# Clearing tiles on ScalarE, mixing whole stores with half-batch stores, and moving the last two output slots to plain transfers

## The chip, the core and the metric

One core of a Trainium2 chip runs the whole program. The metric is device time in microseconds (us) of one execution, as the median of several runs. The granted clock was 1.00 in all of them. Before the change the median was 195.56 us in the first three runs. Of the sixteen DMA engines, which move the data, "landing" means here the moment at which one of them counts its part of a transfer as done; "engine-us" are microseconds summed over the sixteen.

## The reference

The program cuts overlapping 8x8 windows, stride 4, out of 16 images of 64 channels of 64x64 floats. Nothing is computed; it is copying alone.

```python
x: (16, 64, 64, 64) float32            # 16.8 MB read
n_h = n_w = (64 - 8) // 4 + 1          # 15
result: (16, 15, 15, 64, 8, 8)         # 59.0 MB written
for i in range(n_h):
    for j in range(n_w):
        result[:, i, j] = x[:, :, 4*i : 4*i + 8, 4*j : 4*j + 8]
```

Seen as memory, the output is 3600 rows (16 images x 15 x 15 windows) of 16 KB each: one window of one image, all channels.

## The kernel before

The input is loaded once into a tile `L`. Partition `p` holds one half of the channels (`ch`, 64 partitions each), one half of the images (`y`, "half-batch"), one image and one quarter of the rows (`q = p & 3`). A quarter of 16 rows gives four windows, called slots `s` = 0 to 3, for each column `j`. Slot 3 needs four rows of the next partition, which VectorE fetches with a shuffle.

```python
for y in range(NY):                       # loads, 24 in all
    for q in range(HQ):
        load(nc.sync, 0, y, q, SMALL, CL)     # 28 of 32 channels, on SyncE's queue
        load(nc.gpsimd, 0, y, q, 0, SMALL)    # 4 channels, on GpSimd's queue
        load(nc.gpsimd, 1, y, q, 0, CL)       # the other channel half
```

Four tiles `G` of 128 partitions x 16 KB turn. ScalarE (`act`) and VectorE (`dve`) copy windows into one, then GpSimd issues one indirect store of its 128 rows. The row numbers are in an index tile. A row whose index lies out of bounds is dropped.

```python
def scatter(g, ix, j, s):
    st = nc.gpsimd.indirect_dma_start(out=o_v, out_offset=...(ap=ix[:, 0:1]), in_=g..., 
                                      bounds_check=B * NWIN - 1, oob_is_err=False)
...
EARLY = 3
for t in range(NG):                       # clear what a half-store does not fill
    for half in range(CH):
        nc.vector.memset(G[t][...32 partitions..., :, :, :], 0.0)
t = 0
for y in range(NY):                       # half-stores: 64 of 128 rows valid
    for j in range(EARLY):
        ...fill...; scatter(G[t % NG], (idx_y0, idx_y1)[y], j, 0); t += 1

units = [(j, s) for j in range(NW) for s in (0, 2) if s or j >= EARLY]
for j, s in units:
    g = G[t % NG]; t += 1
    if s == 0:                            # "whole" store: slots 0 and 1
        ...; scatter(g, idx, j, s)
    else:                                 # "crossed" store: slots 2 and 3
        turn = j % 2                      # which half of the partitions holds slot 3
        fill(g, turn, s, j, 0, HP, (act, act))
        fill(g, 1 - turn, s + 1, j, 0, HP, (dve, dve))
        scatter(g, (idx_hi, idx_lo)[turn], j, s)
```

Slot 3 of the last quarter does not exist, so a crossed store drops 16 rows. All of them lie in partitions 64 to 127 with `idx_hi` and in 0 to 63 with `idx_lo`.

## Time and profile before

| | before |
|---|---|
| median | 195.56 us (195.54 to 195.88) |
| span of the profiled run | 193.9 us |
| VectorE, ScalarE, GpSimd busy | 68%, 64%, 27% |
| moved | 75.81 MB, 391 GB/s over the span |
| loads end / last 16 KB record ends / span ends | 47.2 / 190.6 / 193.9 us |

The way to read it: no compute engine is near full, and the DMA row is at nine tenths almost throughout. So the useful question is not what a copy costs but where the sixteen DMA engines stand idle. The prediction below shows the lines. Three more matter for what follows. They are SyncE's own waits; the columns are who waited for whom, us in total, times, and the longest. L204 is the end of the program.

```profile
SPq L204 <- DMA out_dram<-G,idx: 160.6, 1, 160.6
SPq L204 <- DMA out_dram<-G,idx_hi: 4.5, 1, 4.5
SPq L204 <- PEq L204: 2.5, 2, 2.0
```

SyncE waits for all stores, and then, in the last line, another 2.0 us for the other engines at the final barrier.

### The profile page before, as it was taken

The numbers are of one execution on the slowest core, as the hardware profiler recorded it, in microseconds if no ns is written. First come the engines' busy times: TensorE is split into PE (matmuls) and PEld (weight loads), VectorE is DVE, ScalarE is ACT, GpSimd is POOL, SyncE is SP. The second block draws the span as 40 slices with busy tenths as digits, with TensorE's granted clock in tenths as the row PEclk, the third lists the DMA queues.
The fourth block names the chain that finished last, engine by engine and source line by source line (L and its number), as shares of the span: only waits on it lengthen the run. The fifth ranks groups of instructions, "written<-read, shape, count | busy, mean of one in ns | idle before, by whom it ended". The sixth has DMA issues, their size and how long they took to land.

```text
span 193.9 us, 478 instructions
## 1 busy us (share of the span) xinstructions
DVE 131.9 (68%) x156; ACT 123.5 (64%) x66; POOL 53.3 (27%) x54
## 2 busy tenths in 40 slices
DVE  6887778995999998766577657774777477643000
ACT  0000008960999999999779677977797779772000
POOL 7402211106463233231404211331323232311000
DMA  2999999999989999999999999999999999999980
GB/s 85 326 408 401 402 399 397 400 400 405 426 333 382 406 419 419 423 423 404 426 433 421 416 419 419 423 423 433 423 416 412 426 423 423 426 416 421 412 345 30
DMA packets 11476, 75.81 MB, mean 391 GB/s; under 512 B 3776, under 2 KB 3776, under 8 KB 7872
## 3 DMA queue, kind: packets, MB, share of 16 engines
q0 software_dynamic: 9616, 68.43, 85.9%
q1 hardware_dynamic: 1856, 7.34, 9.8%
q14 instruction: 4, 0.03, 0.0%
HBM read 16.78 MB, written 69.21 MB: 444 GB/s over the span
## 4 chain that ended last, share of the span: by engine, by line
DMA 66%; DVE 17%; issue 6%; POOL 2%; POOLq 1%; DVEq 0%; PEldq 0%
DMA out_dram<-G,idx 21%; DMA L<-in_x_dram 18%; DMA out_dram<-G,idx_hi 14%; DMA out_dram<-G,idx_lo 12%; DVE G L136 8%; DVE G L139 6%; DVE G L138 3%; POOL L L57 2%; POOLq L204 1%; DVEq L136 0%; POOL pi L68 0%; DVEq L138 0%; PEldq L204 0%
## 5 line engine op out<-in xcount | busy, mean ns | idle before, releaser
L136 ACT COPY G<-L 64x2048 f32<-64x2048 f32 (+1 forms) x65 | 122.2, 1896 | 22.5 <-DMA out_dram<-G,idx 9.9
L136 DVE COPY G<-L 64x2048 f32<-64x2048 f32 (+1 forms) x37 | 44.8, 1221 | 15.6 <-DMA out_dram<-G,idx 12.7
L139 DVE STREAM_SHUFFLE G<-L 64x1024 f32<-64x1024 f32 x30 | 38.3, 1275 | 0.0
L138 DVE COPY G<-L 64x1024 f32<-64x1024 f32 x30 | 20.7, 690 | 20.1 <-DMA out_dram<-G,idx_hi 13.3
L150 DVE MEMSET G<- 32x4096 f32 x8 | 27.8, 3472 | 7.9 <-issue 6.2
L115 POOL DMA_INDIRECT out_dram<-G,idx x12 | 12.4, 1030 | 33.3 <-ACT G L136 33.3
L115 POOL DMA_INDIRECT out_dram<-G,idx_hi x8 | 11.8, 1471 | 31.4 <-DVE G L139 17.8
L136 ACT ACT_TABLE_LOAD x1 | 1.3, 1283 | 29.6 <-DMA L<-in_x_dram 29.6
L57 POOL DMA_DIRECT2D L<-in_x_dram x16 | 9.8, 626 | 25.0 <-DMA L<-in_x_dram 24.4
L115 POOL DMA_INDIRECT out_dram<-G,idx_lo x7 | 9.7, 1390 | 20.5 <-ACT G L136 14.3
L115 POOL DMA_INDIRECT out_dram<-G,idx_y x6 | 9.3, 1547 | 13.7 <-DVE G L136 8.8
L77 DVE TENSOR_TENSOR th<-tc,tq 128x1 int32<-128x1 int32 x2 | 0.3, 159 | 0.1
L77 DVE CUSTOM_DVE_ANT_0 idx_y<-idx,th 128x2 uint16<-128x2 uint16 x2 | 0.3, 158 | 0.1
L74 DVE TENSOR_SCALAR th<-tc 128x1 int32<-128x1 int32 x2 | 0.3, 154 | 0.1
L68 POOL IOTA pi<- 128x1 int32 x1 | 0.1, 125 | 0.4 <-PEq L204 0.4
L139 DVE LOAD_MASK_SELECT G<-L x30 | 0.2, 6 | 0.0
L77 DVE CUSTOM_DVE_ANT_0 idx_hi<-idx,th 128x2 uint16<-128x2 uint16 x1 | 0.2, 159 | 0.0
L77 DVE CUSTOM_DVE_ANT_0 idx_lo<-tb,th 128x2 uint16<-128x2 uint16 x1 | 0.2, 159 | 0.0
L77 DVE CUSTOM_DVE_ANT_0 idx<-tb,th 128x2 uint16<-128x2 uint16 x1 | 0.2, 161 | 0.0
L77 DVE CUSTOM_DVE_ANT_0 idx_lo<-idx_lo,th 128x2 uint16<-128x2 uint16 x1 | 0.2, 158 | 0.0
L77 DVE CUSTOM_DVE_ANT_0 tb<-tb,th 128x2 uint16<-128x2 uint16 x1 | 0.2, 159 | 0.0
L91 DVE TENSOR_SCALAR th<-th 128x1 int32<-128x1 int32 x1 | 0.2, 153 | 0.0
(13 smaller groups left out, 1.7 us busy)
## 6 DMA issues: line engine op xcount, KB each, us to landing
L<-in_x_dram POOLq DMA_DIRECT2D x8, 1024.0 KB, 21.1
L<-in_x_dram SPq DMA_DIRECT2D x8, 896.0 KB
L<-in_x_dram POOLq DMA_DIRECT2D x8, 128.0 KB, 21.3
out_dram<-G,idx POOLq DMA_INDIRECT x12, 14.6
out_dram<-G,idx_hi POOLq DMA_INDIRECT x8, 13.9
out_dram<-G,idx_lo POOLq DMA_INDIRECT x7, 14.1
out_dram<-G,idx_y POOLq DMA_INDIRECT x6, 6.2
```

The lines of the kernel that those rows point to most:

```text
L57: eng.dma_start(out=L[p0 : p0 + QP - HQ + 1 : HQ, c0:c1, :, :], in_=x_v[ch, y, q, :, c0:c1, :])
L68: nc.gpsimd.iota(pi[:, :], pattern=[[0, 1]], base=0, channel_multiplier=1)
L74: nc.vector.tensor_scalar(out=d[:, :], in0=a[:, :], scalar1=float(m), scalar2=None, op0=ALU.mult)
L77: nc.vector.tensor_tensor(out=d[:, :], in0=a[:, :], in1=b[:, :], op=op)
L91: nc.vector.tensor_scalar(out=th[:, :], in0=th[:, :], scalar1=-1.0, scalar2=FAR, op0=ALU.mult, op1=ALU.add)
L115: st = nc.gpsimd.indirect_dma_start(out=o_v, out_offset=bass.IndirectOffsetOnAxis(ap=ix[:, 0:1], axis=0), in_=g.rearrange("p c r w -> p (c ...
L136: copy(out=g[d, cs, :, :], in_=L[f, :, s * ST : s * ST + WS, cols])
L138: copy(out=g[d, cs, 0:ST, :], in_=L[f, :, s * ST : RB, cols])
L139: nc.vector.stream_shuffle(out=g[d, cs, ST:WS, :], in_=L[f, :, 0:ST, cols], mask=nxt)
L150: nc.vector.memset(G[t][p0 : p0 + QP, :, :, :], 0.0)
L204: with _tile.TileContext(nc) as tc:
```

## The change

Three things are meant to save time: free VectorE of 27.8 us of clearing so that the first stores issue earlier; put whole stores between the half-stores of the second half-batch so that the DMA has more to do while ScalarE and VectorE are short of time; and let the last two slots leave as plain transfers from SyncE, sixteen rows at a time. Besides, the choice of the half that drops rows goes from 8 `idx_hi` and 7 `idx_lo` to 9 and 6. (`HWP = 8` covers all loads, so the loads are the same.)

```diff
-    EARLY = 3
-    for t in range(NG):
-        for half in range(CH):
-            nc.vector.memset(G[t][p0 : p0 + QP, :, :, :], 0.0)
+    EARLY = NG - 1
+    zero = ipool.tile([P, 1], f32, name="zero")
+    nc.vector.memset(zero[:, :], 0.0)
+    for g in G:
+        act(out=g.rearrange("p c r w -> p (c r w)"), in_=zero.to_broadcast([P, CFREE]))
...
-            turn = j % 2
+            turn = int(crossed % 5 in (1, 3))
+            crossed += 1
...
+    for j in range(EARLY):
+        part(0, j)
+    plain = [(j, 0) for j in range(EARLY, NW - 1)]
+    cross = [(j, 2) for j in range(NW)]
+    for j in range(EARLY):
+        part(1, j)
+        unit(*plain.pop(0))
+    while plain:
+        for w in cross[:2]:
+            unit(*w)
+        cross = cross[2:]
+        unit(*plain.pop(0))
+
+    j = NW - 1
+    tile_()                                   # one tile is passed over
+    for s in range(2):
+        g = tile_()
+        ...four copies into partitions 32 to 95...
+        for q in range(HQ):
+            free(nc.sync.dma_start(out=o_q[q * NSLOT + s, j], in_=g_q[QP + q : ... : HQ]))
```

More of the change, by code (lines that the diff above doesn't have):

```diff
@@ L50 @@
     x_v = x.rearrange("(y b) (ch cl) (hq r) w -> ch y hq b cl (r w)", y=NY, ch=CH, hq=HQ)
-    SMALL = 4
+    SMALL, HWP = 4, 8
     def load(eng, ch, y, q, c0, c1):
@@ L104 @@
         for q in range(HQ):
-            load(nc.sync, 0, y, q, SMALL, CL)
-            load(nc.gpsimd, 0, y, q, 0, SMALL)
+            hw = y * HQ + q < HWP
+            if hw:
+                load(nc.sync, 0, y, q, SMALL, CL)
+            load(nc.gpsimd, 0, y, q, 0, SMALL if hw else CL)
             load(nc.gpsimd, 1, y, q, 0, CL)
@@ L112, with free @@
     G = [gpool.tile([P, C, WS, WS], f32, name=f"G{n}") for n in range(NG)]
+    o_q = out.rearrange("b i j c r w -> i j b (c r w)")
+    def free(st):
+        tc.declare_no_dep(st.ins, group="stores", reason="each store writes rows of its own")
+        tc.add_to_no_dep_group("stores", st.ins)
     def scatter(g, ix, j, s):
@@ L123, in scatter @@
         )
-        tc.declare_no_dep(st.ins, group="stores", reason="each store writes rows of its own")
-        tc.add_to_no_dep_group("stores", st.ins)
+        free(st)
     def fill(g, half, s, j, lo, n, copies):
@@ L141, with tile_, part, unit @@
     act, dve = nc.scalar.copy, nc.vector.tensor_copy
-    EARLY = 3
-    assert EARLY < NG
-    for t in range(NG):
-        for half in range(CH):
-            p0 = half * HP + (QP if t < EARLY else 0)
-            nc.vector.memset(G[t][p0 : p0 + QP, :, :, :], 0.0)
-    t = 0
-    for y in range(NY):
-        for j in range(EARLY):
-            for half in range(CH):
-                copies = (dve, dve) if y and half and j == 1 else (act, dve)
-                fill(G[t % NG], half, half, j, y * QP, QP, copies)
-            scatter(G[t % NG], (idx_y0, idx_y1)[y], j, 0)
-            t += 1
-    units = [(j, s) for j in range(NW) for s in (0, 2) if s or j >= EARLY]
-    for j, s in units:
-        g = G[t % NG]
-        t += 1
+    EARLY = NG - 1
[3 more added lines that the diff above has]
+        act(out=g.rearrange("p c r w -> p (c r w)"), in_=zero.to_broadcast([P, CFREE]))
+    at = 0
+    def tile_():
+        nonlocal at
+        at += 1
+        return G[(at - 1) % NG]
+    def part(y, j):
+        g = tile_()
+        for half in range(CH):
+            fill(g, half, half, j, y * QP, QP, (dve, dve) if y and half else (act, dve))
+        scatter(g, (idx_y0, idx_y1)[y], j, 0)
+    crossed = 0
+    def unit(j, s):
+        nonlocal crossed
+        g = tile_()
         if s == 0:
             for half in range(CH):
-                fill(g, half, s + half, j, 0, HP, (act, dve))
+                fill(g, half, half, j, 0, HP, (act, dve))
             scatter(g, idx, j, s)
         else:
-            turn = j % 2
+            turn = int(crossed % 5 in (1, 3))
+            crossed += 1
             fill(g, turn, s, j, 0, HP, (act, act))
@@ L173 @@
             scatter(g, (idx_hi, idx_lo)[turn], j, s)
+    for j in range(EARLY):
[13 more added lines that the diff above has]
+    for s in range(2):
+        g = tile_()
+        cols = slice(j * ST, j * ST + WS)
+        for y in range(NY):
+            d = slice(QP + y * QP, QP + (y + 1) * QP)
+            for ch, copy in enumerate((act, dve)):
+                f = slice(ch * HP + y * QP, ch * HP + (y + 1) * QP)
+                copy(out=g[d, ch * CL : (ch + 1) * CL, :, :], in_=L[f, :, s * ST : s * ST + WS, cols])
+        g_q = g.rearrange("p c r w -> p (c r w)")
+        for q in range(HQ):
+            free(nc.sync.dma_start(out=o_q[q * NSLOT + s, j], in_=g_q[QP + q : QP + q + (B - 1) * HQ + 1 : HQ]))
 _INS = ['x', 'window_size', 'stride']
```

## The prediction

> **What bounds the kernel now.** First the page: busy time of the engines, the slices (the DMA row is the mean busy share, in tenths, of the sixteen DMA engines in 40 slices of 4.85 us), and the chain of work that ended last:
>
> ```profile
> DVE 131.9 (68%) x156; ACT 123.5 (64%) x66; POOL 53.3 (27%) x54
> ...
> DMA  2999999999989999999999999999999999999980
> ...
> DMA packets 11476, 75.81 MB, mean 391 GB/s; under 512 B 3776, under 2 KB 3776, under 8 KB 7872
> ...
> DMA 66%; DVE 17%; issue 6%; POOL 2%; POOLq 1%; DVEq 0%; PEldq 0%
> ```
>
> No compute engine passes 68%, and the DMA engines sit at nine tenths from the second slice to the last but one: the kernel is bound by moving 75.8 MB. What is left to win is idle time of the DMA engines, so I next asked the view of windows for DMA share (last column but one; over 1.00 where records overlap) by stage:
>
> ```profile
> 2.30:5.30 3.00, 2.83 (x1) 0.00 (x0) 3.00 (x6) 1.00 0.57 178
> 5.30:47.00 41.70, 33.87 (x34) 12.27 (x7) 8.19 (x13) 1.00 1.04 394
> 47.00:54.00 7.00, 5.85 (x5) 5.95 (x4) 4.00 (x3) 1.00 1.02 424
> 54.00:56.00 2.00, 1.94 (x3) 1.98 (x2) 1.35 (x2) 1.00 0.67 271
> 56.00:73.00 17.00, 16.69 (x25) 16.81 (x10) 5.32 (x5) 1.00 0.96 400
> 73.00:187.00 114.00, 70.13 (x91) 86.52 (x46) 30.29 (x24) 1.00 1.01 421
> 187.00:191.00 4.00, 0.00 (x0) 0.00 (x0) 0.00 (x0) 1.00 0.32 135
> ```
>
> Loads run to 47 us, stores from there. There are only two holes that this change can touch. One is at 54 to 73 us, where ACT and DVE are full (16.8 of 17 us) and the DMA is not. Summing the packet records per microsecond gives 22.5 engine-us missing from 16 engines between 54 and 73 us, that is **1.4 us**. The other is 187 to 191 us, where half the engines have ended.
>
> GpSimd's row of the timeline (start us, us, what, and the idle time before it), then the group of instructions that clears tiles, tell why the second half-batch starves:
>
> ```profile
> 44.53 1.53 POOL L115 DMA_INDIRECT out_dram<-G,idx_y  x1 [8.77 <-DVE G L136]
> ...
> 52.10 2.20 POOL L115 DMA_INDIRECT out_dram<-G,idx_y  x1 [2.70 <-ACT G L136]
> 54.94 1.86 POOL L115 DMA_INDIRECT out_dram<-G,idx_y  x1 [0.65 <-issue]
> 57.74 0.96 POOL L115 DMA_INDIRECT out_dram<-G,idx_y  x1 [0.94 <-ACT G L136]
> 61.59 0.96 POOL L115 DMA_INDIRECT out_dram<-G,idx_hi  x1 [2.88 <-ACT G L136]
> ```
>
> ```profile
> L150 DVE MEMSET G<- 32x4096 f32 x8 | 27.8, 3472 | 7.9 <-issue 6.2 <-PEq L190 1.7
> ```
>
> The first store waits 8.8 us for DVE, which clears tiles until 36.9 us. Three half-stores (64 valid rows of 16 KB, about 2.5 us of DMA each) are followed by stores that come every 3.85 us because ACT fills them.
>
> The tail is in the landing records (sixteen counts per store, one for each DMA engine). At the last store but one, eight engines land at 183.84 to 184.09 us, seven at 185.19 to 185.47, one at 186.19. At the last, a store with dropped rows in partitions 64 to 127, eight land at 187.54 to 187.78, seven at 190.06 to 190.34, one at 191.03. So there are two groups of eight, **a late group and an early group**, and the late one sets the end.
>
> **What the Trainium skill says.** (1) "DMA: Bandwidth & Descriptors", section "Queues, rings and completion order": an engine takes turns between the rows that have work, draining "a whole packet" (about 9 to 17 descriptors) first. The trace differs: on an engine with both queues active the records alternate one by one, a 4-byte or 4096-byte record of the GpSimd queue, then one 4096-byte record (0.16 us) of the SyncE queue. The measurement decides. (2) The same page, section "Why a DMA increments its semaphore by 16 and not by 1": a transfer uses the largest number of engines up to 16 that divides its outermost size, the lowest-numbered ones from SyncE. The trace agrees: the SyncE loads of 8 partitions keep 7.9 engines busy. A store of 16 partitions should then put one row on each engine. (3) The same page, "Issuing engines are not separate DMA queues": issuing from SyncE saves only issue time. So the plain stores bring no bandwidth. (4) "ScalarE: Activation LUTs", "What ACT_TABLE_LOAD costs": a table load is about 1283 ns (here 1283) and an instruction with immediates 186 ns + 0.833 ns per element, 1.89 us at 2048 (here 1896 ns).
>
> **The change part by part.**
>
> *Clearing on ScalarE.* Eight memsets (27.8 us) leave DVE; four copies of 128x4096 come to ACT. No row of before has this size; by the skill's formula 186 + 0.833 x 4096 = 3.6 us each (an estimate), 14.4 in all. With the table load ACT ends near 18 us, before the 29.6 us at which its first data land. The loads' issue is unchanged (all eight still have their SyncE part), so the new clearing is hidden. What it gives: DVE now copies at 29.6 instead of 38.9 us, and the first store can issue at about 37 us (ACT: three copies to 35.2, then 1.9), 7 us earlier. But GpSimd's queue is first in, first out: on the upper engines it carries loads until 47.2 us, on the lower ones its small records alternate with the SyncE loads until 45.4 us and drain after. Stores cannot begin before about 46.7 to 47.2 us, where they begin now. **Worth 0.**
>
> *Whole stores between the second half-batch ones.* All loads are in at 48.0 us, as now. From durations of before (ACT 1.9, DVE 1.22 a copy, a POOL issue about 2, a half-store 2.5 of DMA, a whole one 4.95) I get: half-store 4 issued at 51.8 (three DVE copies from 48.06), flowing 54.2; whole store at 54.3 (its tile is back at 50.3, ACT 3.8 from there), flowing 56.8 behind the half one; half at 58.0 (DMA free for it at 61.7); whole at 60.5 (64.2); half at 64.2 (69.1); whole at 66.7 (71.6); first crossed at 70.7 (76.5). Issue leads need by 2 to 6 us from the second on. A hole of about 0.3 us stays at 54. **Saves 1.4 - 0.3 = 1.1 us.**
>
> *Steady part.* Two crossed stores to one whole: ACT 3 x 3.8 = 11.4 us against DMA 4.33 + 4.33 + 4.95 = 13.6; DVE 3.94 x 2 + 2.5 = 10.4. DMA-bound as before. Worth 0.
>
> *Which half loses rows.* A crossed store drops 16 rows, all in one half of the partitions: two of eight rows on each of eight engines. Before there are 8 that drop in the upper half and 7 in the lower: late group 24 + 96 + 8x8 + 7x6 = 226 rows, early group 224. After it is 9 and 6, with eleven whole stores and 8 rows each of the plain ones: 24 + 88 + 9x8 + 6x6 + 8 = **228** and 222. A row is 0.62 us (3600 records, mean 624 ns), so the late group gains 2 rows: **costs 1.2 us.**
>
> *Plain last stores.* The same 128 rows, one in sixteen on each engine. Counted from the landing of the store three from the end on the late group: refill 3.9, SyncE start 1.6 (its first load: issue 0.75, first record 2.3), so the first four rows come at 5.8 to 7.9, the other four at 10.8 to 12.9, while that group has 16 scattered rows (9.9 us) and these eight (5) to do: 14.9, never dry. The early group idles but ends by about 13.5. Worth 0.
>
> Sum: -1.1 + 1.2 = +0.1 us, 195.7. One late engine slipped 0.65 us beyond its seven peers in before; that it recurs is a coin's toss, so I take 0.3 off.
>
> **Rivals.** *The tail is better than I count.* If the plain rows fall unevenly in favour of the late group, or the crossed order was tuned to an imbalance that the new start creates, then both holes close: 1.1 of supply plus up to 1.3 of tail (half of the 2.6 us between the groups), 193.2. For it: someone chose 9 to 6 on purpose. Against: the records of before show the other sign. *Earlier stores collide with loads.* If stores did enter the lower engines before their SyncE loads end, each 16 KB row would hold up a 4 KB load for 0.62 us, 12 rows 7.4 us; the second half-batch would come up to 5 us late and the DMA run dry: 198 to 200. Against: the queue order above. *ACT becomes the bound*, by 14.4 us more: busy 138 of 194 us, only before 30 us; unlikely. *More lag starves the early group* and nothing else: hidden.
>
> **Range and chances.** I shade the sum toward the first rival by a little: **195.2 us**, range 193.6 to 196.9. Faster by over 2% needs 191.6, more than both holes (1.4 + 1.3) together: 0.03. Slower by over 2% needs 199.5, the collision: 0.03. Within 2%: 0.94.
>
> **What would show it.** The first stores issue at 37 to 43 us but their first 16 KB record still comes at 46.5 to 47.2; the DMA share of 56 to 73 us rises from 0.96 to 1.00; four ACT copies near 3.6 us each before 20 us; in the last landings the two groups lie about 5 us apart, or, with the skill's engine count wrong for the plain stores, do not. A SyncE load landing after 48 us, or a store record before 46 us, makes me wrong on the start; an early group that is not early, on the tail.

## The result

The changed kernel takes **194.8 us** (194.53 to 195.11, 4 runs) against 195.61 (195.54 to 195.88, 4 runs). The ratio is 0.9957, 95% interval 0.9938 to 0.9975. Ratios here are the mean time of one kernel's fast runs over the mean of the other's fast runs of the same rounds, so they are not quite the ratio of the medians quoted. The result is inside the predicted range, and within 2%.

The windows of the changed kernel, to be held against those of before (in each row: busy time of VectorE, ScalarE, GpSimd, then clock, DMA share, GB/s):

```profile
47.00:54.00 7.00, 5.90 (x5) 5.61 (x3) 1.52 (x1) 1.00 1.01 424
54.00:56.00 2.00, 1.94 (x3) 1.98 (x2) 1.36 (x2) 1.00 0.67 271
56.00:73.00 17.00, 15.31 (x18) 14.30 (x9) 8.34 (x6) 1.00 1.00 415
73.00:180.00 107.00, 74.73 (x100) 86.07 (x46) 27.67 (x22) 1.00 1.01 421
180.00:184.00 4.00, 1.39 (x2) 1.59 (x2) 0.00 (x0) 1.00 0.68 285
184.00:187.00 3.00, 1.05 (x1) 2.36 (x2) 0.00 (x0) 1.00 0.72 306
187.00:191.00 4.00, 0.00 (x0) 0.00 (x0) 0.00 (x0) 1.00 0.73 303
```

From 56 to 73 us the share rose from 0.96 to 1.00. At 54 to 56 it did not move: 0.67 in both. And a new stretch of low share is there from 180 us to the end, about 0.7, that the kernel before does not have before 187 us. Its own windows there:

```profile
180.00:184.00 4.00, 0.00 (x0) 0.00 (x0) 0.00 (x0) 1.00 0.99 422
184.00:187.00 3.00, 0.00 (x0) 0.00 (x0) 0.00 (x0) 1.00 1.03 437
```

GpSimd's timeline shows the stores' issue, and the group table shows the clearing:

```profile
37.23 2.08 POOL L124 DMA_INDIRECT out_dram<-G,idx_y  x1 [1.01 <-ACT G L144]
42.16 1.00 POOL L124 DMA_INDIRECT out_dram<-G,idx_y  x1 [2.85 <-DMA L<-in_x_dram]
43.59 0.96 POOL L124 DMA_INDIRECT out_dram<-G,idx_y  x1 [0.43 <-issue]
52.48 1.86 POOL L124 DMA_INDIRECT out_dram<-G,idx_y  x1 [7.93 <-ACT G L144]
54.98 1.86 POOL L124 DMA_INDIRECT out_dram<-G,idx  x1 [0.64 <-issue]
```

```profile
L157 ACT COPY G<-zero 128x4096 f32<-128x4096 f32 x4 | 14.1, 3600 | 0.0
```

The first store issues at 37.2 us instead of 44.5, yet the first 16 KB record starts at 46.58 us in this trace and at 46.67 in the one before. The four clears take 3.6 us each and are over at 16.2 us.

SyncE's own waits:

```profile
SPq L214 <- DVE G L211: 153.7, 1, 153.7
SPq L245 <- DMA out_dram<-G: 2.6, 5, 0.6
SPq L214 <- ACT G L211: 2.2, 2, 1.3
...
SPq L245 <- PEq L245: 0.7, 2, 0.5
```

The wait at the final barrier fell from 2.0 to 0.5 us. This is the surprise. The records of the trace say what it is. GpSimd's last long instruction is a drain (from 176.57 us on before, from 171.47 us on now), and it ends 2.0 us after the last landing *of GpSimd's own queue*, in both kernels. Why it takes these 2.0 us the records do not show. The two kernels side by side, from the landing, packet and instruction records of the two profiled runs (engine-us missing from sixteen, divided by 16, is given as us):

```
                                             before          after      change
idle DMA time, 54 to 73 us                    1.35            0.76       -0.59
rows of the late group                         226             228       +2
last landings, early group (8)      187.54-187.77   190.58-190.68
last landings, late group (7)       190.06-190.34   190.87-191.15       +0.81
last landing of all                         191.02          191.98       +0.96
last landing of GpSimd's queue              191.02          188.52
GpSimd's drain ends                         193.07          190.53
span ends                                   193.87          192.90       -0.97
span's end after the last landing             2.84            0.92       -1.92
```

So the data arrive *later* than before, by 0.96 us, and the program still ends 0.97 us earlier, because the 2 us of drain now pass beside the plain stores. The next part tests this.

### The profile page after: what moved, and what is told of

Its sections match the earlier page's. It is cut to its first block, busy times and chain, and to the rows that moved or that the text cites. A ratio compares the mean times of both kernels' runs of the same rounds, so it can differ in the third digit from the quotient of the medians.

```text
span 192.9 us, 487 instructions
## 1 busy us (share of the span) xinstructions
DVE 110.2 (57%) x153; ACT 138.3 (72%) x70; POOL 54.6 (28%) x53
## 4 chain that ended last, share of the span: by engine, by line
DMA 73%; DVE 12%; issue 7%; POOL 2%; ACTq 1%; ACT 1%; DVEq 0%; PEldq 0%
DMA out_dram<-G,idx 34%; DMA out_dram<-G,idx_hi 22%; DMA L<-in_x_dram 16%; DVE G L144 9%; POOL L L58 2%; DVE G L146 2%; DVE G L147 2%; ACTq L245 1%; ACT G L211 1%; DVEq L144 0%; POOL pi L69 0%; DVEq L146 0%; PEldq L245 0%; ACTq L211 0%
## 5 line engine op out<-in xcount | busy, mean ns | idle before, releaser
L144 ACT COPY G<-L 64x2048 f32<-64x2048 f32 (+1 forms) x61 | 115.3, 1896 | 40.0 <-issue 20.7
L146 DVE COPY G<-L 64x1024 f32<-64x1024 f32 x30 | 21.6, 720 | 21.5 <-DMA out_dram<-G,idx 16.2
L58 POOL DMA_DIRECT2D L<-in_x_dram x16 | 11.4, 715 | 23.9 <-DMA L<-in_x_dram 23.4
L124 POOL DMA_INDIRECT out_dram<-G,idx_lo x6 | 8.9, 1480 | 24.1 <-DVE G L147 17.0
L157 ACT COPY G<-zero 128x4096 f32<-128x4096 f32 x4 | 14.1, 3600 | 0.0
L211 ACT COPY G<-L 32x2048 f32<-32x2048 f32 x4 | 7.6, 1896 | 7.4 <-DMA out_dram<-G,idx 4.9
L211 DVE COPY G<-L 32x2048 f32<-32x2048 f32 x4 | 4.9, 1220 | 10.1 <-DMA out_dram<-G,idx 6.6
```

Of the source, the lines that this page charges most:

```text
L58: eng.dma_start(out=L[p0 : p0 + QP - HQ + 1 : HQ, c0:c1, :, :], in_=x_v[ch, y, q, :, c0:c1, :])
L124: st = nc.gpsimd.indirect_dma_start(out=o_v, out_offset=bass.IndirectOffsetOnAxis(ap=ix[:, 0:1], axis=0), in_=g.rearrange("p c r w -> p (c ...
L144: copy(out=g[d, cs, :, :], in_=L[f, :, s * ST : s * ST + WS, cols])
L146: copy(out=g[d, cs, 0:ST, :], in_=L[f, :, s * ST : RB, cols])
L157: act(out=g.rearrange("p c r w -> p (c r w)"), in_=zero.to_broadcast([P, CFREE]))
L211: copy(out=g[d, ch * CL : (ch + 1) * CL, :, :], in_=L[f, :, s * ST : s * ST + WS, cols])
```

## The experiments

Ten kernels ran, all correct, five runs each (four of before_plain) beside runs of the kernel before on the same chip. The table gives all; the parts follow. Kernels are compared by their ratios.

| label | kernel | median us | before, same call | ratio to before (95%) |
|---|---|---|---|---|
| (the change) | 9 and 6 drops | 194.8 | 195.61 | 0.9957 (0.9938 to 0.9975) |
| turn78 | the change, 7 and 8 drops | 192.69 | 195.85 | 0.9838 (0.9825 to 0.9852) |
| turn69 | the change, 6 and 9 drops | 192.27 | 195.85 | 0.9817 (0.9804 to 0.9831) |
| plain_gps | the change, plain stores from GpSimd | 197.03 | 195.85 | 1.0063 (1.0050 to 1.0077) |
| before_plain | before, plain last stores alone | 193.73 | 195.85 | 0.9891 (0.9876 to 0.9906) |
| before_clear | before, clearing on ScalarE alone | 195.82 | 195.57 | 1.0011 (0.9998 to 1.0025) |
| before_order | the same and the new order | 195.43 | 195.57 | 0.9995 (0.9982 to 1.0009) |
| early4 | turn78, four early half-stores, loop fitted to it | 192.02 | 195.57 | 0.9819 (0.9806 to 0.9833) |
| early4_69 | the same with 6 and 9 drops | 192.03 | 195.57 | 0.9815 (0.9802 to 0.9829) |
| early4_noskip | early4, no tile passed over | 192.06 | 195.62 | 0.9818 (0.9805 to 0.9831) |
| no_lock | the change, two copies as shuffles | 196.85 | 195.62 | 1.0062 (1.0048 to 1.0076) |

### The drain: who issues the last stores

Theory: GpSimd's drain waits for GpSimd's queue, so what counts is which engine issues the last transfers. Rival: the plain form, or the 64 partitions, make the end short.

```diff
-            free(nc.sync.dma_start(out=o_q[q * NSLOT + s, j], in_=...))
+            free(nc.gpsimd.dma_start(out=o_q[q * NSLOT + s, j], in_=...))
```

> The changed kernel with the eight plain stores issued by GpSimd instead of SyncE, nothing else. Drain theory (at the end GpSimd drains its own queue and is done 2.0 us after the last landing of that queue, 191.04 to 193.07 in the kernel before, 188.52 to 190.53 in the changed one; plain stores on SyncE hide that): the 2 us come back, 196.7 us, the span ends 2.8 us after the last landing instead of 0.9. Rival, it is the plain form or the 64 partitions that shorten the end: no change, 194.8.

Measured: 197.03 us, by the ratios 1.06% or 2.1 us more than the changed kernel. The last landing is at 191.97 us, where it is with SyncE (191.98), and the span ends 3.1 us after it, at 195.1. SyncE's waits have the barrier back:

```profile
SPq L245 <- DMA out_dram<-G: 166.5, 1, 166.5
SPq L245 <- PEq L245: 2.4, 2, 1.9
```

The same bytes from the same partitions land at the same time; only the end differs. The rival falls: it is the issuing engine that counts.

The other direction, the kernel before with nothing but its last whole store replaced:

```diff
-    units = [(j, s) for j in range(NW) for s in (0, 2) if s or j >= EARLY]
+    units = [(j, s) for j in range(NW) for s in (0, 2) if s or EARLY <= j < NW - 1]
...
+    (the plain stores of slots 0 and 1 of the last column, as in the change)
```

> The kernel before with only the last part of the change: slot 0 and 1 of the last column by plain stores from partitions 32 to 95, at the end. Drain theory: 226 rows for the late group as before, the end after the last landing falls from 2.8 to 0.9 us: 193.6 us. Rival, the plain stores win nothing by themselves and the gain of the change is all at 54 to 73 us: 195.6.

Measured: 193.73 us, ratio 0.9891, 2.1 us less. Its last landing is at 191.16 us (191.02 before) and its span ends at 192.08. So this part alone is worth more than the whole change. SyncE's wait at the barrier is short here too:

```profile
SPq L223 <- PEq L223: 0.7, 2, 0.5
```

### The rows: which half drops them

If the plain stores win 2.1 us, the whole change 0.8, and the order does not lose (below), something in the change costs more than 1 us. The prediction's candidate is the late group's two extra rows. The test changes one line.

```diff
-            turn = int(crossed % 5 in (1, 3))
+            turn = int(crossed % 2 == 0)             # turn78
+            turn = int(crossed % 5 not in (1, 3))    # turn69
```

> The changed kernel, with only the choice of which half of the partitions loses its rows altered: 7 crossed stores drop rows in partitions 64 to 127 and 8 in 0 to 63 (9 and 6 before). Row theory: the late group has 224 rows instead of 228, 4 x 0.61 = 2.4 us less; the store that frees the tile of the last plain ones lands as much earlier, so the whole tail moves: 192.4 us, and the two groups' counts of the last scattered stores lie about 0.6 us apart instead of 5.4. Rival, the tail is paced by the issue of the plain stores and not by the late group: no change, 194.8.

> As the run before with 6 and 9. Row theory: the late group falls to 222 rows, the early one rises to 228 and becomes the late one, by about 1.9 us at the last crossed store; 228 rows at the faster group's 0.619 us instead of 0.625 end 1.4 us earlier than in the changed kernel: 193.4 us, worse than 7 and 8. Rival, lag is a matter of time and not of rows: the same groups stay late and it is the best of the three.

Measured: 192.69 and 192.27 us. By the ratios, turn78 is 1.2% or 2.3 us below the changed kernel, with 2.4 expected. The landings of the last scattered store and of the last plain one, from the records (two groups of eight engines; "one" is a single engine):

```
            last scattered store                    last plain store
after       180.40-180.57 | 186.56-186.86, 188.52   190.58-190.68 | 190.87-191.15, one 191.98
turn78      183.13-183.26 | 183.81-184.06, 185.96   188.64-188.74 | 188.93-189.21, one 189.98
turn69      182.54-182.79, 184.48 | 185.05-185.20   188.57-188.62, one 188.75 | 189.33-189.45
```

In the changed kernel one group stood 6 us ahead at its last scattered store and then could do nothing but wait for plain rows, which is the share of 0.7 from 180 us on. With 7 and 8 drops the groups are 0.8 us apart, and the windows of turn78 show the stretch nearly full:

```profile
180.00:184.00 4.00, 1.69 (x2) 3.19 (x2) 0.00 (x0) 1.00 0.94 395
184.00:187.00 3.00, 0.00 (x0) 0.00 (x0) 0.00 (x0) 1.00 0.94 393
```

With 6 and 9 the order of the groups is turned round, and the straggler, one engine of the group that serves partitions 0 to 63, is now in the early group where it costs nothing. My expectation of turn69 (193.4) missed by 1.1 us, of which 0.8 is that straggler, which I had left out: it ends 0.8 us after its seven peers in the first two kernels, and is hidden in the third. Rows decide which group is late, since the groups change places. But rows are not the whole lag. Six rows are 3.7 us (0.624 us each); the medians of the two groups at the last scattered store lay 6.3 us apart in the changed kernel and 2.4 us the other way round in turn69. So the group of partitions 0 to 63 loses a further 1.4 to 2.5 us that its rows do not explain. The rival, a lag that comes with time, is thus not wholly out: its forecast that the same group stays late failed, and its forecast that 6 and 9 is the best of the three came true.

### The start: clearing and order

```diff
-            nc.vector.memset(G[t][p0 : p0 + QP, :, :, :], 0.0)
+        act(out=g..., in_=zero.to_broadcast([P, CFREE]))       # before_clear
```

> The kernel before with only the clearing moved to ScalarE (four copies of a zero, 128x4096 each). Prediction's step: the first stores issue at 37 to 44 us instead of 44.5 to 49.4 but queue behind the loads, the first 16 KB record stays at 46.5 to 47.2 us, worth 0: 195.8 us. Rival, the earlier issue keeps the DMA engines fuller at the change from loads to stores: 195.2 or less.

Measured: 1.0011 (0.9998 to 1.0025), nothing gained. The first store issues at 37.4 us and the first 16 KB record comes at 46.51 us. The step "worth 0" holds.

```diff
+    for j in range(EARLY):
+        mixed += [(1, j, None), (j + EARLY, 0)]      # half-store, whole store
...
+    while whole or cross:
+        mixed += cross[:2] + whole[:1]
```

This kernel, before_order, has the clearing and the order of the change, all stores scattered, and 8 and 7 drops.

> The kernel before with the clearing on ScalarE and the new order of stores, all of them scattered, 8 and 7 crossed drops (226 rows for the late group, as before). Prediction's step was 1.1 us; the trace of the changed kernel shows the idle time between 54 and 73 us fall from 1.35 to 0.76 us, so the order is worth 0.6: 195.2 us. Rival, the order is worth nothing because the tail is longer for it: 195.8.

Measured: 0.9995, that is 0.3 us below before_clear in the same rounds, and no clear gain over the kernel before. This is half of what I expected. The idle time between 54 and 73 us did fall to 0.76 us, from 1.37 in before_clear. But the two groups, with the same 226 and 224 rows, end 3.3 us apart (186.49 to 186.64 and 189.70 to 189.96), against 2.5 in before_clear (187.72 to 187.89 and 190.19 to 190.50): the early group came 1.2 us earlier, the late one, which sets the end, only 0.4. Why the lag grew with this order is open.

### The hole at 54 us

The prediction had 0.3 us of idle left there; 0.63 us (10.1 engine-us in the one microsecond at 54) was left. Two tests.

The first asks for the cause of the slow issue: 1.86 us, where others take 0.96. The Trainium skill, "SBUF — State Buffer", section "SBUF: two separate sides", says that GpSimd cannot write descriptors while VectorE runs a two-port copy, and calls it "The "DVE blocks DMA" trap". In the changed kernel VectorE copies back to back from 47.98 to 66.7 us.

```diff
+    def same(out, in_):
+        nc.vector.stream_shuffle(out=out, in_=in_, mask=list(range(32)))
...
-                fill(g, half, half, j, 0, HP, (act, dve))
+                fill(g, half, half, j, 0, HP, (act, same if j == EARLY else dve))
```

> The changed kernel with VectorE's two copies of the first whole store (64x2048) made by a shuffle with the identity mask, which is slower (about 2.5 us each). Blocking theory: GpSimd's issue of the first store of the second half-batch ends 0.1 us after the start of a VectorE copy (54.34 us, copies at 51.7, 53.0, 54.2) because back-to-back VectorE copies keep GpSimd out; with shuffles after 51.7 us it starts at 51.8 and takes 0.96 instead of 1.86 us, and the 10 engine-us missing at 54 us fall to 3 or fewer. The whole store comes 2.6 us later, so a hole at 57 us opens and the time stays within 0.3 us of 194.8. Rival, the issue is slow for another reason: it still ends after 54 us.

Measured, from its timeline and its windows:

```profile
51.69 2.41 DVE L154 STREAM_SHUFFLE G<-L 64x2048 f32<-64x2048 f32 x1
52.42 0.96 POOL L124 DMA_INDIRECT out_dram<-G,idx_y  x1 [7.95 <-ACT G L144]
...
57.32 1.86 POOL L124 DMA_INDIRECT out_dram<-G,idx  x1 [3.94 <-DVE G L154]
```

```profile
54.00:56.00 2.00, 1.96 (x3) 1.98 (x2) 0.00 (x0) 1.00 1.03 426
56.00:58.00 2.00, 1.94 (x3) 1.98 (x2) 0.68 (x1) 1.00 0.21 90
58.00:60.00 2.00, 1.97 (x2) 1.98 (x2) 1.19 (x1) 1.00 0.31 131
```

The issue beside shuffles takes 0.96 us and the hole at 54 is gone (share 1.03), which is what the page leads one to expect. It starts at 52.4 and not at 51.8 us: about 0.75 us pass between the end of the last copy (51.65) and the issue, which my plan had counted as 0.1. The second half of the expectation missed. The time is 196.85, not within 0.3 of 194.8: the whole store came at 57.3 us, its issue beside copies took 1.86 again, and a hole of 3.1 us opened from 56 to 60. That hole is 2.3 us more than the changed kernel's, and the kernel is 2.05 us slower by the ratios. So this idle DMA time turned into time nearly one to one, where the 0.6 us saved in before_order gave only half.

The second test removes the hole by having more stores ready, a fourth half-store of the first half-batch. It takes the drops of turn78, and the loop that mixes crossed and whole stores now takes three crossed ones in a turn where needed, as two whole stores fewer are left for it (6 instead of 8):

```diff
-    EARLY = NG - 1
+    EARLY = NG
...
-    while plain:
-        for w in cross[:2]:
+    while plain or cross:
+        n = 2 + (len(cross) > 2 * len(plain))
+        for w in cross[:n]:
```

> The kernel with 7 and 8 drops, and a fourth half-store of the first half-batch ahead of the second half-batch, so that the DMA has 10 us of stores instead of 7.5 when the last loads land at 48 us. Theory: what is left of the hole (10 of 12.2 engine-us lie in the microsecond at 54) is the time to make the first store of the second half-batch, and goes: 0.6 us less, 192.1 us. Rival, the hole moves to 57 us since the next tile is only free when the first store has landed at 50.2: 192.7.

> The same with 6 and 9 drops. If the end is set by one engine of the lower group that is 0.8 to 1.2 us behind its seven peers (189.98 against 189.2 with 7 and 8, hidden with 6 and 9), it is 0.4 us better than the run before, 191.7; if by the groups alone, it is worse, 192.7.

Measured: 192.02 and 192.03 us. The idle time in early4 fell from 0.85 us (turn78) to 0.42, and the ratio from 0.9838 to 0.9819, which is 0.4 us. The two intervals overlap, so this gain is not clear of the noise. What idle time remains lies at 56 to 59 us, where the rival placed it. In early4_69 the idle time was 0.93 us (12.8 engine-us of it at 56 and 57 us), which may be where the gain of the hidden straggler was lost; the two expectations for it both missed. Neither kernel is clear of turn69 (0.9817), which has no fourth half-store.

Last, the tile that the change passes over before its plain stores:

```diff
     j = NW - 1
-    tile_()
```

> The kernel with four early half-stores and 7 and 8 drops, without the tile that is passed over before the plain stores, so these take the two tiles that come free first and can issue one store (some 4.5 us) earlier. Theory: what is left of idle time in the tail (5.6 engine-us between 183 and 187 us, 0.35 us) is waiting for the plain stores' tiles, and goes: 191.7 us. Rival, the tail is set by the late group's rows, whose engines never waited: 192.0, no change.

Measured: 192.06 us, no change. The plain stores' tiles are not what the end waits for. The late group ended at 188.34 to 188.60 us with one engine at 189.28, and with the tile passed over at 188.47 to 188.74 and 189.23.

## Why the prediction was right or wrong

The range and the class were right. The sum behind them was not: one term was missing 1.9 us, another was too large by 0.5 to 0.8, and the time came out inside the range because these missed in opposite directions. That is luck, not a working that held.

- **Clearing worth 0: right**, by before_clear (1.0011). The durations were right too: 3.6 us each, over at 16.2 us (18 predicted).
- **"Saves 1.4 - 0.3 = 1.1 us" by the order: right in kind, too large.** The idle time went from 1.35 us (the prediction summed 1.4) to 0.76, so 0.6 was saved. The term that was mis-sized is "issued at 51.8", the first store of the second half-batch: its issue started at 52.48, because 0.75 us pass between the last copy and the issue, and every issue up to the first crossed store, at 71.39 for 70.7, came 0.7 to 0.8 us late. The lead from there to the flow was right: 2.4 us forecast (51.8 to 54.2), 2.45 measured (52.48 to 54.93). And of the 0.6 us only 0.3 reached the clock in before_order, where the groups ended further apart.
- **"The late group gains 2 rows: costs 1.2 us": right.** The late group's landings came 0.81 us later although 0.59 us of idle time was gone, together 1.4. The turn of the drops in turn78 gave 2.3 us back for four rows, which is close to the slope assumed (2.5).
- **"Plain last stores. Worth 0": wrong.** This is the step that failed. I followed the data to the last row and stopped there. The span ended 2.84 us after the last landing before, and 0.92 us after it now. The term is 1.9 us, shown by plain_gps (+2.1 us when GpSimd issues them) and by before_plain (-2.1 us for this part alone). The line that would have told me was in the trace of before: SyncE's 2.0 us at the final barrier. What the step says of the data held: the late group's engines did not run dry between the last scattered store (186.56 to 186.86 us) and the last plain one.
- **The straggler.** I called its return a coin's toss and took 0.3 us off. It was 0.7 us behind its peers before and 0.83 after, and it is there near the end of all twelve traces (see the last section).
- **The rival "the tail is better than I count"** named the right place and the wrong cause. The order of drops was not tuned to a hidden imbalance; it was simply worse, and 6 and 9 or 7 and 8 beat it by over 2 us.
- **The sign "two groups about 5 us apart in the last landings": wrong place.** They were 6.3 us apart at the last scattered store and 0.4 at the last plain one, since the early group had to wait for its plain rows. The skill's engine count was not at fault: the sixteen landings of the last plain store all lie between 190.58 and 191.98 us. (The 7.9 busy engines that the prediction reads for the SyncE loads hold from 8 to 13 us; from 5.3 to 45.4 us the mean is 7.0.)
- The collision of early stores with loads did not occur: the first store record came at 46.58 us, the last load record ended at 47.22, both as before.

The best versions, turn69, early4, early4_69 and early4_noskip, are equal within the noise (0.9815 to 0.9819, 192.0 to 192.3 us) and beat both kernels. The first of them is the changed kernel with one line altered.

## What to carry to other kernels

Where the DMA is the bound, account for the end of the program as well as for its bytes: see which engine's drain ends last, and let the last transfers leave from an engine that adds little after them (here SyncE, 0.9 us to the end of the span, for GpSimd 2.8 to 3.1). Count rows per DMA engine and not in total, since here the rows dropped in one half of the partitions made the eight engines of the other half late, and the late ones set the end. A range that holds because two errors cancel is no proof of the working, so each term has to be checked in the trace by itself.

## What the Trainium skill lacked or had wrong

- "DMA: Bandwidth & Descriptors", section "Queues, rings and completion order", has an engine drain a whole packet, typically about 9 to 17 descriptors, before it changes queue. In the trace of the kernel before, between 13 and 15 us, the records of the engines with both queues active seem to alternate one by one: one of 4 bytes or 4096 bytes from GpSimd's queue, one of 4096 bytes from SyncE's. The records carry no engine number, so this is read from how their times join, and they do not tell where a packet ends. If a record was a packet here, the page's rule held and only its typical size did not fit; the prediction's "the trace differs" says more than is shown.
- No page that I read has the 2.0 us of GpSimd's final drain after the last landing of its own queue (191.02 to 193.07, 188.52 to 190.53 and, with 2.3 us, 191.97 to 194.30), nor that it is hidden when the last stores are another engine's. The DMA page's 2 us of fixed cost per DMA (section "Anatomy of one DMA — SWDGE (gpsimd) path") is told as lying before the completion count, and this one lies after it.
- No page that I read has what GpSimd's loads of 8 partitions leave in the records: one record of 4 bytes for each data record. The count fits: 3712 records of 4 bytes on GpSimd's queue are 2304 such fillers (as many as its 4096-byte records), 624 dropped rows and 784 completions (33 stores and 16 loads, sixteen each). That the fillers lie on the engines without data is not shown.
- The DMA page, section "Latency and other measured facts", has engines 7 and 15 usually slower. What it lacks is a lag of eight of the sixteen, the ones that serve partitions 0 to 63. In the kernel before, at stores after which both groups had had equally many rows, the medians of the two groups' landings lay 0.1 us apart at 105 us and 1.35 us at 179 us; with the new order (before_order) it was 2.0 us at 173 us. The cause is open.
- No page that I read has the straggler, one engine of that group. In all twelve traces four records of 8 KB on the instruction queue (0.31 us each) fall among the stores, and soon after most of them one engine lands behind its seven peers; after the last one, which starts between 169.9 and 181.1 us, it does so in every trace, by 0.7 to 1.7 us. That the fetch is the cause was not tested, and whether this engine is the page's engine 7 the trace does not tell.
- "SBUF — State Buffer", section "SBUF: two separate sides", is borne out: 1.86 us for an issue beside back-to-back VectorE copies, 0.96 beside shuffles. What the page does not give is the size: all five issues of 1.86 us up to 67 us in the changed kernel end 0.09 to 0.10 us after a VectorE copy has started (54.24 and 54.34, 56.75 and 56.84, and so on).
